# Two fused transformer blocks: the wide levels of a gated recurrence taken from keys and queries decayed once per chunk, and the key factor entered into the exponent as a logarithm

## The chip, the cores and the metric

The kernel runs on one core of one Trainium2 chip, as one program. Its engines work side by side and each takes its own instructions in the order of its own list: TensorE (PE; its weight loads are shown as PEld), VectorE (DVE), ScalarE (ACT), GpSimd (POOL) and SyncE (SP), which issues most transfers. The metric is the device time of one execution in microseconds (us), as the median over runs; smaller is better.

## The reference, cut to what matters

Two blocks of a transformer follow each other on 512 tokens of width 1024. The second block has a mixer with two halves: four heads of a gated recurrence (HGRN2, 128 features each) and eight heads of stick-breaking attention (64 features each).

```python
f = lbf + (1.0 - lbf) * sigmoid(f_logit)      # forget gate, per token and feature
k = 1.0 - f
bc = cumsum(log(f))                           # within chunks of 64 tokens
def step(state, inp):                         # one chunk
    qt, kt, vt, bt = inp
    decay = exp(where(causal, bt[t] - bt[s], -inf))
    a = einsum('td,sd,tsd->ts', qt, kt, decay)
    o_intra = a @ vt
    o_inter = (qt * exp(bt)) @ state
    b_last = bt[-1]
    new_state = exp(b_last)[:, None] * state + (kt * exp(b_last - bt)).T @ vt
    return new_state, o_intra + o_inter
```

The stick-breaking heads need `exp(log_sigmoid(z) + between)`, where `between` is a sum of logarithms taken backwards along the keys. Both halves are normalised per head, joined to `mixed`, and multiplied by `w_out`; a memory attention and a feed-forward layer follow.

## The kernel before

The kernel has no running state. For a head of the recurrence it writes the whole 512x512 matrix of scores as a sum over **levels**: at level hl the tokens are cut into blocks of 2*hl, and the scores of the upper half of a block against its lower half are one small product of decayed queries and decayed keys, both measured from the last token of the lower half. The levels are 1, 2, 4, 8, 16, 32 (inside a chunk), 64 (two neighbouring chunks), 128 and 256 (the wide ones, across chunks), and level 0 for the diagonal. `b` is the cumulative sum of log f within a chunk, written over `f` (tile q), with features on the 128 partitions and the 512 tokens along a row.

For a level up to 64, `exponents` (L1410) has POOL subtract for the lower half (L1417) and for the upper half (L1419), then `decayed` (L1400) has ACT take the exponential of the whole tile (L1407) and DVE multiply the lower half by the key factor kf (L1408) and the upper half by the query (L1409). For a wide level, `far_exponents` (L1431) first adds up chunk totals on POOL in single columns (L1438 to L1443), subtracts on POOL (L1448, L1450), and goes through the same exponential and products. `scores` (L1455) does the products on PE (L1460 for the diagonal, L1468 up to level 64, L1481 and L1487 for 128 and 256), and DVE and ACT fold the results into tiles that `hgrn_tail` (L1497) multiplies with the values.

Around this run the projections of the mixer ("fills": 256 columns of w_in each, three matmuls per product, since the weights and activations are split in a high part, cast on ACT at L403, and a low part, subtracted on DVE at L404), the stick-breaking heads (`sb_head`: PE L616, DVE L1556 to L1566, ACT L1560, L1561, L1567, transposes L756, products L1575), and the product with w_out (`fill_part`), which begins while the last two heads are still at their levels. `fill_part` splits four finished head outputs (tiles y) into high and low parts (tiles h) and then multiplies.

PE's order is written out by hand: `weave` (L653) goes through all of this as generators, asks a small planner with due times which step is ready (each step names its PE time and the chain of DVE, ACT and POOL work behind it, in `prepared`, `first` and `after`), and PE takes the steps in that order. `prepare` runs LOOK + 1 = 3 levels ahead of `scores`. The orders of DVE, ACT and POOL are chosen by the scheduler of the tile framework when the program is built, and are fixed from then on. Tiles w come from a pool of 16, PSUM banks b from a pool of 6.

Of the kernel before, what the change touches and what calls it, by code (L numbers as in the profile page):

```python
# [11 lines left out]
F32 = mybir.dt.float32  # L12
F32R = mybir.dt.float32r
U8 = mybir.dt.uint8
AF = mybir.ActivationFunctionType
ALU = mybir.AluOpType
AX = mybir.AxisListType

P = 128
S = 512  # L20
D = 1024
# [9 lines left out]
LEVELS = (32, 16, 8, 4, 2, 1)  # L31
# [63 lines left out]
def transformer_blocks_kernel(  # L95
# [41 lines left out]
    V, A, G, T = nc.vector, nc.scalar, nc.gpsimd, nc.tensor  # L137

    cp = ctx.enter_context(tc.tile_pool(name="cp", bufs=1))
# [7 lines left out]
    def nm(s):  # L147
        uid[0] += 1
        return f"{s}_{uid[0]}"
# [13 lines left out]
    def wt(dt=F32):  # L163
        return big("w", WBUFS, dt)
# [7 lines left out]
    def col(n=4, bufs=20):  # L172
        return sp.tile([P, n], F32, tag=f"c{n}", bufs=bufs, name=nm("c"))
# [383 lines left out]
    with tc.high_priority(2 * WPRIO):  # L557
        pre = PreNorm("mix_pre")
        with in_order({}):
            rs = []  # L560
            for t in range(5):
                if t < 4:
                    su = [squares(xt[t, 0]), col(1)]
                    V.tensor_tensor_reduce(out=junk2, in0=xt[t, 1], in1=xt[t, 1], scale=1.0 / D, scalar=0.0,
                                           op0=ALU.mult, op1=ALU.add, accum_out=su[1])
# [646 lines left out]
    for hl in (64,) + LEVELS:  # L1212
        nb = 64 // hl
# [15 lines left out]
    V.memset(ones_sb, 0.0)  # L1229
    V.memset(ones_sb[0:64, 0:64], 1.0 / 64)  # L1230
    V.memset(ones_sb[64:128, 64:128], 1.0 / 64)
    small = cp.tile([P, 2], F32, name="small")
    V.memset(small[:, 0:1], 1e-30)
    V.memset(small[:, 1:2], 1e-6)
    tiny, eps6 = small[:, 0:1], small[:, 1:2]


    def pools(first, second, mid):
# [145 lines left out]
    def hgrn_chain(hd):  # L1384
        q, f = store["q", hd], store["f", hd]
        yield STEP()
        kf = wt()
        A.activation(kf, f, AF.Copy, scale=-1.0, bias=1.0)
        A.activation(f, f, AF.Ln, bias=tiny)
        b = f  # L1390
        V.tensor_tensor_scan(out=b, data0=reset, data1=f, initial=0.0, op0=ALU.mult, op1=ALU.add)

        bc = b.rearrange("p (c t) -> p c t", t=64)
        tot = bc[:, :, 63]

        def halves(t, hl):
            v = t.rearrange("p (b u c) -> p b u c", u=2, c=hl)
            return v[:, :, 0, :], v[:, :, 1, :]

        def decayed(e, hl):  # L1400

            el, eu = halves(e, hl)
            if hl == 64:
                A.activation(el, el, AF.Exp)
                A.activation(eu, halves(b, hl)[1], AF.Exp)
            else:
                A.activation(e, e, AF.Exp)  # L1407
            V.tensor_tensor(el, el, halves(kf, hl)[0], op=ALU.mult)  # L1408
            V.tensor_tensor(eu, eu, halves(q, hl)[1], op=ALU.mult)  # L1409

        def exponents(hl):
            e = wt()
            el, eu = halves(e, hl)
            bl, bu = halves(b, hl)
            nb = 256 // hl
            ref = bl[:, :, hl - 1:hl].to_broadcast([P, nb, hl])
            G.tensor_tensor(el, ref, bl, op=ALU.subtract)  # L1417
            if hl != 64:
                G.tensor_tensor(eu, bu, ref, op=ALU.subtract)  # L1419
            decayed(e, hl)  # L1420
            return e

        ad = wt()

        w0, w13, w2 = [wt(F32R) for b in range(2)], [wt(F32R) for b in range(2)], wt(F32R)
        w2 = [w2[:, :256], w2[:, 256:]]

        def diagonals(t):
            return t.rearrange("p (a c) -> p a c", c=P)[:, 0:4:3]

        def far_exponents(hl):  # L1431
            nch = hl // 64
            nb = 256 // hl
            lowc, upc = col(8), col(8)
            tv = tot.rearrange("p (b u c) -> p b u c", u=2, c=nch)
            lv = lowc[:, :4].rearrange("p (b c) -> p b c", c=nch)
            uv = upc[:, :4].rearrange("p (b c) -> p b c", c=nch)
            G.tensor_copy(lv[:, :, nch - 1], tv[:, :, 0, nch - 1])  # L1438
            G.memset(uv[:, :, 0:1], 0.0)
            for c in range(nch - 1):  # L1440
                G.tensor_tensor(lv[:, :, nch - 2 - c], lv[:, :, nch - 1 - c],
                                tv[:, :, 0, nch - 2 - c], op=ALU.add)
                G.tensor_tensor(uv[:, :, c + 1], uv[:, :, c], tv[:, :, 1, c], op=ALU.add)  # L1443
            e = wt()
            ev = e.rearrange("p (b u c t) -> p b u c t", u=2, c=nch, t=64)
            bv = b.rearrange("p (b u c t) -> p b u c t", u=2, c=nch, t=64)
            for bb in range(nb):
                G.tensor_tensor(ev[:, bb, 0], lv[:, bb].unsqueeze(2).to_broadcast([P, nch, 64]),  # L1448
                                bv[:, bb, 0], op=ALU.subtract)
                G.tensor_tensor(ev[:, bb, 1], uv[:, bb].unsqueeze(2).to_broadcast([P, nch, 64]),  # L1450
                                bv[:, bb, 1], op=ALU.add)
            decayed(e, hl)
            return e

        def scores(hl, e):  # L1455
            ps = aux()
            if hl == 0:
                for gg in range(4):
                    sl = slice(gg * P, (gg + 1) * P)
                    T.matmul(ps[:, sl], kf[:, sl], q[:, sl], start=True, stop=True)  # L1460
                V.tensor_tensor(ad.rearrange("p (g t) -> p g t", g=4),
                                ps.rearrange("p (g t) -> p g t", g=4),
                                ident.unsqueeze(1).to_broadcast([P, 4, P]), op=ALU.mult)
                return 0.43
            if hl <= 64:
                for gg in range(4):
                    up = e[:, gg * P:(gg + 1) * P].rearrange("p (b u c) -> p b u c", u=2, c=hl)[:, :, 1, :]
                    T.matmul(ps[:, gg * 64:(gg + 1) * 64], e[:, gg * P:(gg + 1) * P], up,  # L1468
                             start=True, stop=True)
                V.copy_predicated(  # L1470
                    halves(ad, hl)[1],
                    masks[hl].rearrange("p (b c) -> p b c", c=hl),
                    ps[:, :256].rearrange("p (b c) -> p b c", c=hl))
                if hl == 1:
                    split(w0[0][:, :P], w0[1][:, :P], ad[:, :P])
                    split(*[diagonals(t) for t in w13], ad.rearrange("p (a c) -> p a c", c=P)[:, 1:4:2])
                    split(w2[0][:, :P], w2[1][:, :P], ad[:, 256:256 + P])
                return 0.21
            if hl == 128:
                for bb in range(2):  # L1480
                    T.matmul(ps[:, bb * P:(bb + 1) * P], e[:, bb * 256:bb * 256 + P],  # L1481
                             e[:, bb * 256 + P:bb * 256 + 256], start=True, stop=True)
                for bb, t in enumerate((w0, w2)):
                    split(t[0][:, P:256], t[1][:, P:256], ps[:, bb * P:(bb + 1) * P])
            else:
                for bb in range(2):
                    T.matmul(ps[:, bb * 256:(bb + 1) * 256], e[:, bb * P:(bb + 1) * P],  # L1487
                             e[:, 256:512], start=True, stop=True)
                split(w0[0][:, 256:], w0[1][:, 256:], ps[:, :256])
                split(w13[0][:, P:384], w13[1][:, P:384], ps[:, 256:])  # L1490
            return 0.22 if hl == 128 else 0.86

        order = (0, 64) + LEVELS + (128, 256)
        es = {0: None}

        def prepare(n):
            if n < len(order):  # L1497
                hl = order[n]
                es[hl] = far_exponents(hl) if hl > 64 else exponents(hl)

        def prepared(n):
            if n >= len(order):
                return ()
            far = order[n] > 64
            return (("G", 2.3),) * far + (("G", 0.7), ("G", 0.7)) * (not far) + (("A", 0.55), ("D", 0.7))

        first = (("A", 0.6), ("A", 0.6), ("D", 0.6))
        for n in range(1, LOOK + 1):
            prepare(n)
            first += prepared(n)  # L1510
        yield STEP(ops=(first,), lat=TLAT[2], need=1)
        for n, hl in enumerate(order):
            prepare(n + LOOK + 1)
            pe = scores(hl, es.pop(hl))
            after = {0: (("D", 0.6),), 1: (("D", 0.35), ("A", 0.7), ("D", 0.75)), 128: (("A", 0.32), ("D", 0.4)),
                     256: (("A", 0.55), ("D", 0.7))}.get(hl, (("D", 0.35),))
            last = n == len(order) - 1
            yield STEP(pe=pe, ops=(after, prepared(n + LOOK + 1)), lat=HLAT, need=int(not last), free=1,
                       back=0 if last else HBACK)
        store["w", hd] = w0, [t[:, :384] for t in w13], w2, [t[:, 384:] for t in w13]  # L1520
# [352 lines left out]
```

## Time and profile before

| | us |
|---|---|
| median of 3 runs | 1911.21 |
| lowest, highest | 1910.41, 1911.87 |
| the profiled execution's own time | 1912.74 |
| its span, first to last instruction | 1911.0 |
| PE busy over the span | 1881.5 (98%) |
| DVE, ACT, POOL busy over the span | 1388.6, 929.8, 174.9 |

The recurrent heads are worked on between about 1205 and 1410 us of the span. A matmul is counted as busy from its start to its modelled end, and matmuls overlap, so PE's busy share says little on how fast it moves; the time from one start to the next does. In a row of the timeline the first number is the start, the second the duration, and idle time ahead of an instruction stands in brackets with what ended it.

### The profile page before, as it was taken

The numbers are of one execution on the slowest core, as the hardware profiler recorded it, in microseconds if no ns is written. First come the engines' busy times: TensorE is split into PE (matmuls) and PEld (weight loads), VectorE is DVE, ScalarE is ACT, GpSimd is POOL, SyncE is SP. The second block draws the span as 40 slices with busy tenths as digits, with TensorE's granted clock in tenths as the row PEclk, the third lists the DMA queues.
The fourth block names the chain that finished last, engine by engine and source line by source line (L and its number), as shares of the span: only waits on it lengthen the run. The fifth ranks groups of instructions, "written<-read, shape, count | busy, mean of one in ns | idle before, by whom it ended". The sixth has DMA issues, their size and how long they took to land.

```text
span 1911.0 us, 29337 instructions
## 1 busy us (share of the span) xinstructions
PE 1881.5 (98%) x11566; PEld 1688.3 (88%) x11566; DVE 1388.6 (73%) x2217; ACT 929.8 (49%) x1537; POOL 174.9 (9%) x272
## 2 busy tenths in 40 slices
PE   8999999999999999999999999999999999999998
PEld 6899888888999998899999988888888778999997
DVE  6777635468878786777877757888976448878785
ACT  5666534364544445443434356657565344344443
POOL 2330100060000002000000010430410000000000
PEclk9999999999999999999999999999999999999999
DMA  5212224452233324423232342121343222232322
GB/s 180 67 55 68 78 66 154 166 176 89 89 111 96 120 93 162 143 67 111 90 119 99 114 160 71 63 94 39 103 152 133 77 85 82 99 111 89 111 88 89
DMA packets 164908, 198.69 MB, mean 104 GB/s; under 512 B 7745, under 2 KB 131746, under 8 KB 164770
## 3 DMA queue, kind: packets, MB, share of 16 engines
q1 hardware_dynamic: 163202, 192.10, 30.8%
q0 software_dynamic: 1280, 4.20, 0.6%
q8 instruction: 91, 1.49, 0.3%
q10 hardware_dynamic: 288, 0.52, 0.1%
q14 instruction: 47, 0.39, 0.1%
HBM read 186.30 MB, written 10.49 MB: 103 GB/s over the span
## 4 chain that ended last, share of the span: by engine, by line
PE 87%; issue 5%; DVE 3%; ACT 2%; POOL 1%; DMA 1%; SPq 0%; POOLq 0%; DVEq 0%; ACTq 0%
PE b L372 15%; PE b L374 15%; PE b L373 15%; PE a L372 11%; PE a L374 11%; PE a L373 11%; PE a L514 4%; PE b L616 1%; DVE wl L404 1%; PE b L490 1%; PE b L756 1%; PE b L1468 1%; PE b L1774 1%; DMA q<-mact_d 0%; PE b L886 0%
## 5 line engine op out<-in xcount | busy, mean ns | idle before, releaser
L404 DVE TENSOR_TENSOR wl<-wr,wh 128x1024 fp32r<-128x1024 f32 (+1 forms) x381 | 463.0, 1218 | 272.9 <-ACT wh L403 266.4
L403 ACT CAST wh<-wr 128x1024 fp32r<-128x1024 f32 (+1 forms) x381 | 394.1, 1036 | 443.9 <-PE b L373 144.1
L372 PE MATMUL b<-wh,q 128*128 128x512 f32 x672 | 262.4, 390 | 0.0
L373 PE MATMUL b<-wl,q 128*128 128x512 f32 x672 | 262.0, 390 | 0.0
L374 PE MATMUL b<-wh,q 128*128 128x512 f32 x664 | 258.2, 389 | 0.0
L372 PE MATMUL a<-h,wh 128*128 128x512 f32 (+1 forms) x660 | 238.4, 361 | 0.0
L374 PE MATMUL a<-h,wl 128*128 128x512 f32 (+1 forms) x660 | 234.9, 356 | 0.0
L373 PE MATMUL a<-h,wh 128*128 128x512 f32 (+1 forms) x660 | 234.7, 356 | 0.0
L373 PE MATMUL b<-h,wh 128*128 128x256 f32 (+1 forms) x568 | 175.9, 310 | 0.0
L372 PE MATMUL b<-h,wh 128*128 128x256 f32 (+1 forms) x568 | 175.9, 310 | 0.0
L374 PE MATMUL b<-h,wl 128*128 128x256 f32 (+1 forms) x568 | 175.9, 310 | 0.0
L374 PEld LDWEIGHTS b<-wh,q 128*128 128x128 f32 x664 | 124.6, 188 | 26.6
L372 PEld LDWEIGHTS b<-wh,q 128*128 128x128 f32 x672 | 126.3, 188 | 24.6
L373 PEld LDWEIGHTS b<-wl,q 128*128 128x128 f32 x672 | 126.3, 188 | 24.3
L373 PE MATMUL a<-s,wh 128*128 128x256 f32 (+1 forms) x488 | 141.2, 289 | 0.0
L374 PEld LDWEIGHTS a<-h,wl 128*128 128x128 f32 x660 | 124.6, 189 | 18.3
L372 PEld LDWEIGHTS a<-h,wh 128*128 128x128 f32 x660 | 124.7, 189 | 17.9 <-issue 0.5
L373 PEld LDWEIGHTS a<-h,wh 128*128 128x128 f32 x660 | 124.7, 189 | 17.8 <-issue 0.5
L373 PEld LDWEIGHTS b<-h,wh 128*128 128x128 f32 x568 | 108.3, 191 | 5.6
L374 PEld LDWEIGHTS b<-h,wl 128*128 128x128 f32 x568 | 108.2, 191 | 5.6
L372 PEld LDWEIGHTS b<-h,wh 128*128 128x128 f32 x568 | 108.1, 190 | 5.6
L374 PE MATMUL a<-wh,h 128*128 128x256 f32 x368 | 106.6, 290 | 4.5 <-DVE h L404 4.5
(379 smaller groups left out, 4179.7 us busy)
## 6 DMA issues: line engine op xcount, KB each, us to landing
wr<-in_ffn_w_gu_dram SPq DMA_DIRECT2D x88, 512.0 KB
wr<-in_w_in_dram SPq DMA_DIRECT2D x68, 512.0 KB
wr<-in_ffn_w_down_dram SPq DMA_DIRECT2D x44, 512.0 KB
wr<-in_w_gate_dram SPq DMA_DIRECT2D x22, 512.0 KB
wr<-in_w_up_dram SPq DMA_DIRECT2D x22, 512.0 KB
wr<-in_w_down_dram SPq DMA_DIRECT2D x22, 512.0 KB
wr<-in_mem_w_kv_dram SPq DMA_DIRECT2D x16, 512.0 KB
wr<-in_w_out_dram SPq DMA_DIRECT2D x10, 512.0 KB
```

The lines of the kernel that those rows point to most:

```text
L372: T.matmul(ps, lh, rh, start=first, stop=False)
L373: T.matmul(ps, lh, rl, start=False, stop=False)
L374: T.matmul(ps, ll, rh, start=False, stop=last)
L403: A.copy(hi, src)
L404: V.tensor_tensor(lo, src, f32(hi), op=ALU.subtract)
L490: T.transpose(banks[k][:, t * P:(t + 1) * P], self.s[t, k // 4][:, (k % 4) * P:(k % 4 + 1) * P], ident)
L514: T.matmul(accs[m], lh, rh, start=c == 0 and n in (0, 2), stop=c == KT - 1 and n > 3)
L616: T.matmul(ps, lh[n], rh[n], start=n == 0, stop=n == 1)
L756: T.transpose(ps[:, o * P:(o + 1) * P], blk, ident)
L1468: T.matmul(ps[:, gg * 64:(gg + 1) * 64], e[:, gg * P:(gg + 1) * P], up, start=True, stop=True)
L1774: T.matmul(po, lh, rh, start=n == 0, stop=n == 5)
```

## The change

The key factor is no longer multiplied in. ACT takes log(kf) once per head, DVE subtracts it from b once (tile bk), and the lower half's exponent is taken from bk instead of b, so one exponential gives the decayed key and a level has one product on DVE, for the query.

Level 64 is now built in `decayed` from whole chunks: keys decayed to the end of their chunk (kd, one POOL subtraction of 512 columns, one exponential) and queries decayed from the start of theirs (q times exp(b), both in place). The wide levels multiply those by products of whole-chunk decays (`ways`, two short scans on DVE behind two copies on POOL), on DVE alone. The order of the levels moves 64 from behind the diagonal to behind level 1, and the planner's chains are rewritten to match.

```diff
-        kf = wt()
+        bk, kf = wt(), wt()
         A.activation(kf, f, AF.Copy, scale=-1.0, bias=1.0)
         A.activation(f, f, AF.Ln, bias=tiny)
+        A.activation(bk, kf, AF.Ln, bias=tiny)
         b = f
         V.tensor_tensor_scan(out=b, data0=reset, data1=f, initial=0.0, op0=ALU.mult, op1=ALU.add)
+        V.tensor_tensor(bk, b, bk, op=ALU.subtract)
...
-            G.tensor_tensor(el, ref, bl, op=ALU.subtract)
-            if hl != 64:
-                G.tensor_tensor(eu, bu, ref, op=ALU.subtract)
-            decayed(e, hl)
+            G.tensor_tensor(el, ref, halves(bk, hl)[0], op=ALU.subtract)
+            G.tensor_tensor(eu, bu, ref, op=ALU.subtract)
+            A.activation(e, e, AF.Exp)
+            V.tensor_tensor(eu, eu, halves(q, hl)[1], op=ALU.mult)
             return e
...
-        def far_exponents(hl):
...
+        def decayed():
+            kd = wt()
+            G.tensor_tensor(kd.rearrange("p (c t) -> p c t", t=64), tot.unsqueeze(2).to_broadcast([P, 8, 64]),
+                            bk.rearrange("p (c t) -> p c t", t=64), op=ALU.subtract)
+            A.activation(b, b, AF.Exp)
+            A.activation(kd, kd, AF.Exp)
+            V.tensor_tensor(q, q, b, op=ALU.mult)
+            ways = col(16, 4)
+            G.memset(ways, 1.0)
+            G.tensor_copy(ways[:, 0:4:2], tot[:, 1:6:4])
+            G.tensor_copy(ways[:, 5:8:2], tot[:, 2:7:4])
+            for dst, src in ((ways[:, 8:11][:, ::-1], tot[:, 1:4][:, ::-1]), (ways[:, 13:16], tot[:, 4:7])):
+                V.tensor_tensor_scan(out=dst, data0=src, data1=zero.to_broadcast([P, 3]), initial=1.0,
+                                     op0=ALU.mult, op1=ALU.add)
+            base.append((kd, ways))
+            return kd
+        def far(hl):
+            nb, nch = 256 // hl, hl // 64
+            e, (kd, ways) = wt(), base[0]
+            ev, kv, qv = [t.rearrange("p (b u c t) -> p b u c t", u=2, c=nch, t=64) for t in (e, kd, q)]
+            o = 4 * nch - 8
+            for u, v in enumerate((kv, qv)):
+                w = ways[:, o + u * 4:o + u * 4 + 4].rearrange("p (b c) -> p b c", c=nch)
+                for bb in range(nb):
+                    V.tensor_tensor(ev[:, bb, u], v[:, bb, u], w[:, bb].unsqueeze(2).to_broadcast([P, nch, 64]),
+                                    op=ALU.mult)
             return e
...
-        order = (0, 64) + LEVELS + (128, 256)
+        order = (0,) + LEVELS + (64, 128, 256)
...
-            return (("G", 2.3),) * far + (("G", 0.7), ("G", 0.7)) * (not far) + (("A", 0.55), ("D", 0.7))
-        first = (("A", 0.6), ("A", 0.6), ("D", 0.6))
+            if order[n] > 64:
+                return ("D", 1.1),
+            if order[n] == 64:
+                return ("G", 1.3), ("A", 0.6), ("A", 0.6), ("D", 0.7)
+            return ("G", 0.7), ("G", 0.7), ("A", 0.6), ("D", 0.45)
+        first = (("A", 0.6), ("A", 0.6), ("A", 0.6), ("D", 1.2), ("D", 0.7))
```

The lists of DVE, ACT and POOL change between the first head and the end of the mixer, and so does PE's; outside of that stretch the engines' instructions are the same. From here on "the first, second, third and fourth head" are the four recurrent heads in their order.

The first place is DVE's list where `fill_part` begins. `h<-y` is the low part of a finished head output, `q<-reset,q` the cumulative sum of the fourth head, `q<-a` the low part of a value projection, `wl` that of weights. Before:

```order
L404 TENSOR_TENSOR h_13642<-y_12039,h_13641 128x512
L404 TENSOR_TENSOR h_13646<-y_12146,h_13645 128x512
L404 TENSOR_TENSOR wl_13762<-wr_13759,wh_13761 128x512
L404 TENSOR_TENSOR h_13650<-y_12138,h_13649 128x512
L404 TENSOR_TENSOR wl_13768<-wr_13765,wh_13767 128x512
L404 TENSOR_TENSOR q_13636<-a_13552,q_13635 128x256
L1556 SCALAR_TENSOR_TENSOR w_13602<-b_13601,consts 128x128
L1559 TENSOR_SCALAR w_13602<-b_13601 128x384
L404 TENSOR_TENSOR q_13636<-a_13552,q_13635 128x256
L404 TENSOR_TENSOR h_13654<-y_12880,h_13653 128x512
L1564 SCALAR_TENSOR_TENSOR w_13603<-ones_c,w_13603 128x512
L1391 SCALAR_TENSOR_TENSOR q_13107<-reset,q_13107 128x512
```

The same place in the changed kernel, from the second of the four on (L1395 is the new subtraction that gives bk, L1413 the product with the query for levels 32 and 16 of the fourth head):

```order
L404 TENSOR_TENSOR h_13609<-y_12147,h_13608 128x512
L404 TENSOR_TENSOR wl_13695<-wr_13692,wh_13694 128x512
L404 TENSOR_TENSOR q_13599<-a_13537,q_13598 128x256
L1393 SCALAR_TENSOR_TENSOR q_13080<-reset,q_13080 128x512
L404 TENSOR_TENSOR q_13599<-a_13537,q_13598 128x256
L1395 TENSOR_TENSOR w_13508<-q_13080,w_13508 128x512
L404 TENSOR_TENSOR h_13613<-y_12139,h_13612 128x512
L1563 SCALAR_TENSOR_TENSOR w_13587<-b_13586,consts 128x128
L1566 TENSOR_SCALAR w_13587<-b_13586 128x384
L1413 TENSOR_TENSOR w_13521<-w_13521,q_13186 128x8x32
L1413 TENSOR_TENSOR w_13526<-w_13526,q_13186 128x16x16
L404 TENSOR_TENSOR h_13617<-y_12824,h_13616 128x512
```

The cumulative sum of the fourth head, which stood behind the last of the four low parts, now stands between the second and the third, and two products of that head stand ahead of the fourth.

The second place is ACT's list at the same point, where `h<-y` is the high part (the cast). Before:

```order
L1560 ACTIVATE w_13530<-w_13529 128x384
L1561 ACTIVATE w_13530<-w_13530 128x384
L403 CAST h_13641<-y_12039 128x512
L403 CAST h_13645<-y_12146 128x512
L403 CAST wh_13761<-wr_13759 128x512
L1567 ACTIVATE w_13529<-w_13529 128x384
L403 CAST h_13649<-y_12138 128x512
L403 CAST wh_13767<-wr_13765 128x512
L403 CAST q_13635<-a_13552 128x256
L403 CAST h_13653<-y_12880 128x512
```

In the changed kernel (L1412 is the exponential of a level, here 32 and 16 of the third head; L1389 gives kf of the fourth head, L1390 and L1391 its two logarithms):

```order
L403 CAST h_13604<-y_12040 128x512
L1412 ACTIVATE w_13474<-w_13474 128x512
L1412 ACTIVATE w_13479<-w_13479 128x512
L403 CAST wh_13688<-wr_13686 128x512
L1389 ACTIVATE w_13509<-q_13080 128x512
L403 CAST h_13608<-y_12147 128x512
L403 CAST wh_13694<-wr_13692 128x512
L403 CAST q_13598<-a_13537 128x256
L1390 ACTIVATE q_13080<-q_13080,small 128x512
L1391 ACTIVATE w_13508<-w_13509,small 128x512
L403 CAST q_13598<-a_13537 128x256
L403 CAST h_13612<-y_12139 128x512
```

Two exponentials of the third head now stand between the first and the second cast, and the two logarithms of the fourth head between the second and the third.

The third place is PE's list at the end of the second head: L1487 and L1491 are its widest level, 256; the products into one bank b from tiles w and q are those with the values, `hgrn_tail`. Before, a projection (bank a) of 24 matmuls follows level 256, and the first eight rows are:

```order
L1481 MATMUL b_12869<-w_12760 128x128 x2
L1365 MATMUL b_12876<-w_12798,consts 128x512
L1365 MATMUL b_12882<-w_12853,consts 128x512
L1487 MATMUL b_12888<-w_12816 128x256 x2
L372 MATMUL a_12907<-h_11363,wh_12782 128x512
L373 MATMUL a_12907<-h_11364,wh_12782 128x512
L374 MATMUL a_12907<-h_11363,wl_12783 128x512
L372 MATMUL a_12907<-h_11367,wh_12782 128x512
```

In the changed kernel:

```order
L374 MATMUL a_12793<-h_11416,wl_12727 128x512
L1491 MATMUL b_12880<-w_12811 128x256 x2
L1366 MATMUL b_12887<-w_12857,consts 128x512
L372 MATMUL b_12905<-w_12233,q_12272 128x512
L373 MATMUL b_12905<-w_12234,q_12272 128x512
L374 MATMUL b_12905<-w_12233,q_12273 128x512
L372 MATMUL b_12905<-w_12235,q_12272 128x384
L373 MATMUL b_12905<-w_12236,q_12272 128x384
```

The products with the values now begin one matmul (a norm's, L1366) behind level 256, whose scores they need; before, a whole projection lay between.

## Rows read from the trace of the kernel before

**Rows 1.** The page's first part: busy us, share of the span, instructions.

```profile
PE 1881.5 (98%) x11566; PEld 1688.3 (88%) x11566; DVE 1388.6 (73%) x2217; ACT 929.8 (49%) x1537; POOL 174.9 (9%) x272
```

**Rows 2.** Windows: length, busy of PE, PEld, DVE, ACT, POOL, clock, DMA.

```profile
1205.00:1235.00 30.00, 29.43 (x197) 26.76 (x196) 22.84 (x38) 19.34 (x36) 17.09 (x38) 1.00 0.22 71
1235.00:1240.00 5.00, 3.31 (x20) 2.20 (x17) 4.84 (x10) 4.30 (x8) 2.05 (x3) 1.00 0.00 0
1240.00:1339.00 99.00, 99.00 (x609) 88.09 (x609) 83.82 (x161) 68.95 (x134) 18.62 (x37) 1.00 0.19 65
1339.00:1347.00 8.00, 4.07 (x22) 2.84 (x21) 6.94 (x13) 6.61 (x15) 0.00 (x0) 0.88 0.27 78
1347.00:1352.00 5.00, 5.00 (x26) 5.00 (x26) 4.81 (x6) 1.68 (x5) 2.41 (x4) 0.51 1.02 364
1352.00:1398.00 46.00, 46.00 (x380) 45.07 (x378) 41.22 (x84) 23.16 (x44) 24.64 (x44) 1.00 0.29 91
1398.00:1410.00 12.00, 11.16 (x75) 9.73 (x74) 9.37 (x22) 8.05 (x17) 0.00 (x0) 1.00 0.23 72
sum 205.00, PE 197.96 PEld 179.69 DVE 173.84 ACT 132.08 POOL 64.82; mean PE 28.28 PEld 25.67 DVE 24.83 ACT 18.87 POOL 9.26
```

**Rows 3.** Waits of PE, 1205 to 1410: total us, times, longest.

```profile
PE a L374 <- DVE h L404: 4.5, 4, 1.9
PE b L756 <- ACT w L1567: 1.4, 1, 1.4
```

**Rows 4.** Timeline of PE where fill_part begins: start, duration, instruction, idle before.

```profile
1339.45 0.63 PE L616 MATMUL b<-s,q 128*128 128x512 f32 x2
1340.34 0.38 PE L372 MATMUL a<-wh,h 128*128 128x256 f32 x1 [0.26 <-ACT h L403]
...
1346.35 0.58 PE L374 MATMUL a<-wh,h 128*128 128x256 f32 x1 [1.92 <-DVE h L404]
```

**Rows 5.** Timeline of DVE: the third head's cumulative sum.

```profile
1333.03 1.22 DVE L1391 TENSOR_TENSOR_SCAN q<-reset,q 128x512 f32<-128x512 f32 x1
```

**Rows 6.** Groups by form, 1205 to 1410: busy us, mean ns, idle before.

```profile
L1417 POOL TENSOR_TENSOR w<-q 128x256 f32<-128x256 f32 x28 | 21.6, 778 | 200.1 <-DVE q L1391 94.9 <-PE b L1365 72.3 <-PE b L1468 13.0
L1407 ACT ACTIVATE w<-w 128x512 f32<-128x512 f32 x32 | 20.1, 632 | 22.9 <-POOL w L1419 11.7 <-POOL w L1450 7.8 <-PE a L374 3.3
L1409 DVE TENSOR_TENSOR w<-w,q 128x256 f32<-128x256 f32 x36 | 19.8, 549 | 0.7 <-ACT w L1405 0.7
L1419 POOL TENSOR_TENSOR w<-q 128x256 f32<-128x256 f32 x24 | 19.5, 813 | 0.0
L1408 DVE TENSOR_TENSOR w<-w,w 128x256 f32<-128x256 f32 x36 | 19.2, 534 | 8.8 <-ACT w L1407 7.1 <-ACT w L1404 1.4
L1365 PE MATMUL b<-w,consts 128*128 128x512 f32 x16 | 8.2, 602 | 0.6 <-ACT w L1584 0.6
L1391 DVE TENSOR_TENSOR_SCAN q<-reset,q 128x512 f32<-128x512 f32 x4 | 4.8, 1212 | 0.0
L404 DVE TENSOR_TENSOR h<-y,h 128x512 fp32r<-128x512 f32 x6 | 4.1, 698 | 0.0
L403 ACT CAST h<-y 128x512 fp32r<-128x512 f32 x6 | 3.6, 613 | 2.3 <-PE a L373 1.5 <-DVE y L1588 0.8
L403 ACT CAST q<-a 128x256 fp32r<-128x256 f32 x8 | 2.9, 362 | 2.0 <-DVE q L404 2.0
L1389 ACT ACTIVATE q<-q,small 128x512 f32<-128x512 f32 x4 | 2.9, 714 | 0.0
```

**Rows 7.** Timeline: one DVE product with POOL at work, one with POOL idle.

```profile
1231.27 0.80 POOL L1417 TENSOR_TENSOR w<-q 128x256 f32<-128x256 f32 x1
1231.52 0.83 DVE L1409 TENSOR_TENSOR w<-w,q 128x256 f32<-128x256 f32 x1
...
1254.28 0.42 DVE L1409 TENSOR_TENSOR w<-w,q 128x256 f32<-128x256 f32 x1
```

**Rows 8.** Timeline of SP near the end of the mixer.

```profile
1412.34 0.50 SPq L1089 DMA_DIRECT2D q<-mact_d  x1
```

More of the change, by code (lines that the diff above doesn't have):

```diff
@@ L1231, in transformer_blocks_kernel @@
     V.memset(ones_sb[64:128, 64:128], 1.0 / 64)
-    small = cp.tile([P, 2], F32, name="small")
+    small = cp.tile([P, 3], F32, name="small")
     V.memset(small[:, 0:1], 1e-30)
     V.memset(small[:, 1:2], 1e-6)
-    tiny, eps6 = small[:, 0:1], small[:, 1:2]
+    V.memset(small[:, 2:3], 0.0)
+    tiny, eps6, zero = [small[:, k:k + 1] for k in range(3)]
     def pools(first, second, mid):
@@ L1398, in halves @@
             return v[:, :, 0, :], v[:, :, 1, :]
[L1400 to L1409, printed above, removed]
         def exponents(hl):
@@ L1429, in diagonals @@
             return t.rearrange("p (a c) -> p a c", c=P)[:, 0:4:3]
-        def far_exponents(hl):
[L1432 to L1452, printed above, removed]
@@ new lines, in hgrn_chain @@
+        base = []
+        def far(hl):
[8 more added lines that the diff above has]
+                                    op=ALU.mult)
@@ L1465, in scores @@
             if hl <= 64:
+                high = q if hl == 64 else e
                 for gg in range(4):
-                    up = e[:, gg * P:(gg + 1) * P].rearrange("p (b u c) -> p b u c", u=2, c=hl)[:, :, 1, :]
+                    up = high[:, gg * P:(gg + 1) * P].rearrange("p (b u c) -> p b u c", u=2, c=hl)[:, :, 1, :]
                     T.matmul(ps[:, gg * 64:(gg + 1) * 64], e[:, gg * P:(gg + 1) * P], up,
@@ L1473, in scores @@
                     ps[:, :256].rearrange("p (b c) -> p b c", c=hl))
-                if hl == 1:
+                if hl == 64:
                     split(w0[0][:, :P], w0[1][:, :P], ad[:, :P])
@@ L1498, in prepare @@
                 hl = order[n]
-                es[hl] = far_exponents(hl) if hl > 64 else exponents(hl)
+                es[hl] = far(hl) if hl > 64 else exponents(hl) if hl < 64 else decayed()
         def prepared(n):
@@ L1503, in prepared @@
                 return ()
-            far = order[n] > 64
-            return (("G", 2.3),) * far + (("G", 0.7), ("G", 0.7)) * (not far) + (("A", 0.55), ("D", 0.7))
-        first = (("A", 0.6), ("A", 0.6), ("D", 0.6))
+            if order[n] > 64:
[4 more added lines that the diff above has]
+        first = (("A", 0.6), ("A", 0.6), ("A", 0.6), ("D", 1.2), ("D", 0.7))
         for n in range(1, LOOK + 1):
@@ L1514, in hgrn_chain @@
             pe = scores(hl, es.pop(hl))
-            after = {0: (("D", 0.6),), 1: (("D", 0.35), ("A", 0.7), ("D", 0.75)), 128: (("A", 0.32), ("D", 0.4)),
+            after = {0: (("D", 0.6),), 64: (("D", 0.35), ("A", 0.7), ("D", 0.75)), 128: (("A", 0.32), ("D", 0.4)),
                      256: (("A", 0.55), ("D", 0.7))}.get(hl, (("D", 0.35),))
```

## The prediction

> **What bounds the kernel now.** I read the page's busy times first: PE is busy 98% of the span, DVE 73%, ACT 49%, POOL 9% [rows 1]. So an engine other than PE costs time only where PE waits for it, and the question is how much PE waits in the stretch that the change touches. The windows from 1205 to 1410 us answer that [rows 2]: PE is busy 197.96 of 205 us there, DVE 173.84, ACT 132.08, POOL 64.82, and the idle time lies in three places. Between 1235 and 1240 PE is busy 3.31 of 5 us; between 1339 and 1347 it starts 22 matmuls in 8 us; between 1398 and 1410 it is idle 0.84 us. The list of PE's waits [rows 3] names two releasers: the low parts h from DVE, 4.5 us in four waits, and one 1.4 us wait on the stick-breaking product of ACT (that is the place at 1235). No wait names a level's exponent, so the work that the change removes stands nowhere in front of PE.
>
> One more thing is to be seen in the windows. Right behind the long wait the granted clock is 0.51, the lower of its two levels, from 1347 to 1352, and 26 matmuls take 5 us, 0.192 each; between 1352 and 1398 at full clock 380 take 46 us, 0.121 each [rows 2]. The waits at `fill_part` cost twice, once as 8.0 − 22 × 0.121 = 5.3 us of lost starts and once as 26 × 0.071 = 1.8 us of slow matmuls: about 7.
>
> **The change part by part.**
>
> *Work taken away or added, beside PE.* DVE loses 72 products of 256 columns, 19.8 + 19.2 = 39.0 us [rows 6]. It gets 24 products for the query at 0.549 (13.2), four subtractions for bk and four products q times exp(b) of 512 columns at 0.698 as a low part has (5.6), 16 level-128 products of 128 columns and 8 of 256. No row shows those of 128 columns with a broadcast factor: they lie between nothing and 0.549, and I take half, 0.28 (4.4), with 8 × 0.549 (4.4). Eight scans of three columns lie between nothing and the 1.212 of a 512-column scan; I take 0.3 (2.4). Sum 30.0, 9 us less. POOL keeps 48 subtractions at 0.80 (38), gets four of 512 columns at twice 0.80 (6.4; between once and three times) and a dozen small ones (under 3): some 47 against 64.8, 18 less. ACT keeps 32 exponentials of 0.632, loses 8 of half the size (between 0.362, the cast of that width, and 0.632) and gets four logarithms at 0.714 [rows 6]: even within 2 us. All of it lies beside PE, whose instructions stay the same in number and kind, so by itself it is worth nothing; the price is in where it waits. In SP's list one reload for the memory attention, issued at 1412.34 [rows 8], moves behind a pair of weight loads at the very end: between nothing and 1 us, and I take nothing, for PE then has the rest of the mixer before it. The w tiles: bk and kd live through a head where kf did, one more of 16; DVE or POOL could wait for a free one, which I take as nothing and put in the last rival.
>
> *fill_part.* This is the large term. Before, PE comes to it at 1340.34 and gets the matmul that needs the last low part at 1346.35 [rows 4]. After, the last low part on DVE stands behind the fourth head's cumulative sum, its bk and its products for levels 32 and 16; the cumulative sum stands behind the logarithm on ACT, which stands behind the second cast, and that behind two exponentials of the third head, which wait for POOL. A chain over three engines has come in front of PE. I follow it from the third head's cumulative sum, which before begins at 1333.03 [rows 5]. After, a second logarithm and a stick-breaking scan come ahead of it; I put the end of its bk at 1338.8 (an estimate; from the old place it would be 1333.03 + 1.21 + 0.70 = 1334.9). Then POOL's subtraction 0.78 (its partner does not need bk and goes first), POOL's pair for level 16 at 1.6 beside the exponential of level 32, the exponential of level 16 at 0.63: 1341.8. ACT: a weight cast, kf and the second cast h at 0.61 each, 1343.6; another weight cast, 0.36 for q, the logarithm 0.71: 1345.3. DVE: cumulative sum 1.21, a 256-column low part 0.35 (half of 0.698), bk 0.70: 1347.6. POOL 0.8 and 1.6, ACT 0.63, DVE's last product 0.55 and at last the low part 0.70: 1351.9, with the durations of [rows 6]. Against 1346.35 that is 5.5 later. The bounds: if all the early part were in time, what is left hangs on PE's own value projection, whose end lies behind the matmul at 1339.45 [rows 4], about 1340.1; from there 0.36 + 0.35 + 0.70 + 0.8 + 1.6 + 0.63 + 0.55 + 0.70 = 5.7 gives 1345.8, 0.6 earlier than before. Upwards, two further POOL or ACT operations in the wrong place (0.8 + 0.63 each) make it 8. I take 5.5, since the queue orders say which instruction stands behind which. While the low part waits, everything behind it on DVE waits too: the stick-breaking scan and the next levels, for which PE has the rest of fill_part in hand. The slow clock behind the wait I leave at its 1.8 us; it could vanish or double.
>
> *The second head's end.* Before, 24 projection matmuls of 512 columns lie between level 256 and the products with the values (24 × 2 × 0.121, an estimate of 5.8 us). After, one norm matmul of 0.60 does. The products of the second group of rows need level 256's scores cast on ACT (0.36), with a low part on DVE (0.35), and ACT has a copy, two operations of the norm (one waits for that very norm matmul) and a cast in front: 0.6 + 3 × 0.63 + 0.36 + 0.36 + 0.35 = 3.6. PE covers that with the norm matmul and three to five products, 0.6 + 5 × 0.24 = 1.8. Loss 1.8; between nothing and 3.
>
> *Small ones.* The wait at 1235, idle 1.7 us, has one more product of the second head ahead of it: +0.5 (0 to 1). The norm matmul behind the stick-breaking tail comes earlier against its square: +0.4 (0 to 0.8). The idle 0.84 us behind 1398 goes, since the fourth head's last levels there now need DVE alone: −0.8 (0 to −0.84). What is late next there is the cast of the scores, which has the old place.
>
> Sum: 5.5 + 1.8 + 0.5 + 0.4 − 0.8 = 7.4. The profiled execution took 1912.74 with a span of 1911.0; it would take 1920.1. It lies 1.5 above the median of the runs shown, so the forecast on the median is 1911.2 + 7.4 = 1918.6.
>
> *A rule against this.* One product of 256 columns took 0.83 us on DVE while POOL subtracted, and 0.42 while POOL was idle [rows 7]; the mean of 36 is 0.549 [rows 6]. The Trainium skill, page "SBUF — State Buffer", section "Who interferes with whom", says that a VectorE instruction with two SBUF inputs contends with a GpSimd instruction that reads SBUF, and that whichever comes first holds the shared pair of ports to its end. The trace agrees in those two rows. By that rule 18 us less on POOL would free up to as much on DVE, twice my 9 us; as PE waits for DVE at one place only, this changes no term above but makes the second rival below likelier than the order alone would.
>
> **The rivals.**
>
> *Only what hangs on PE counts (no change).* The third head's early part is in time after all, as the scheduler saw it, and fill_part ends 0.6 earlier: −0.6 + 1.8 + 0.5 + 0.4 − 0.8 = +1.3, 1912.5. For it: POOL is busy only 17 of 30 us even in its densest stretch [rows 2]. Against it: the two exponentials now ahead of the second cast wait for POOL, where none did.
>
> *The waits go (faster).* The relief on DVE lets the low parts follow PE at once. Then the 5.3 at fill_part, the 1.8 of slow clock, the 1.7 at 1235 and the 0.8 at 1398 all go: −9.6, 1901.6. It decides if the last low part is ready before 1341. For it: DVE is busy 6.94 of the 8 us of that window [rows 2], so work taken off it there counts. Against it: the low part is behind more of the head's work, not less, and the chain from 1340.1 alone is longer.
>
> *A longer stall (slower still).* The fill_part chain takes its upper 8, the slow clock doubles (+1.8), the second head's end takes 3 and a wait for a w tile adds 1: 8 + 1.8 + 3 + 0.5 + 0.4 + 1 − 0.8 = +13.9, 1925.1. For it: the clock fell behind a 4.5 us wait before, and a 10 us one is longer. Against it: each step must come out at its bad end.
>
> **How the numbers follow.** The forecast has 0.52, no change 0.20, the waits that go 0.15, the longer stall 0.13. The forecast's own range is 1914 to 1922. For eight times in ten the range takes in the no-change case, most of the longer stall and the upper edge of the faster one: 1905 to 1925. About 0.2%, 3.8 us, is what a measurement of this kernel can tell from no change: below 1907.4 counts as faster, above 1915.0 as slower. Faster: the third case, and a little of the second, 0.17. Same: most of the second and the low edge of the forecast, 0.22. Slower: 0.61.
>
> **What would show it.** In the changed profile the waits of PE should name the low part h at fill_part with 9 to 12 us of lost starts instead of 5.3, with DVE's cumulative sum of the fourth head and two level products just ahead of the last low part, and a stretch at half clock behind it. The second head's products with the values should show a wait of 1 to 3 us on a low part of the scores. DVE should be busy about 9 us less and POOL 18 less over the mixer, with PE's busy count unchanged. The prediction is wrong if the last low part ends by 1346, or if the clock stays up.

## The result and the profile after

| | before | changed |
|---|---|---|
| median, us | 1911.11 (6 runs) | 1925.57 (6 runs) |
| lowest to highest | 1910.27 to 1913.03 | 1922.88 to 1927.17 |
| the profiled execution, its span | 1912.74, 1911.0 | 1926.3, 1924.6 |

The changed kernel is slower by a ratio of 1.0073, with a 95% interval of 1.0060 to 1.0086: 14.5 us, where 7.4 were forecast and the range ended at 1925.0. The direction was right, the size half of what came. The rival called "a longer stall" gave 1925.1, but for reasons that were only partly those that happened.

The work went as forecast. The page's first part of the changed kernel, to be held against [rows 1]:

```profile
PE 1886.5 (98%) x11566; PEld 1692.0 (88%) x11566; DVE 1381.5 (72%) x2210; ACT 927.9 (48%) x1533; POOL 158.4 (8%) x212
```

DVE lost 7.1 us (9 were forecast), POOL 16.5 (18), ACT 1.9 (even); PE has the same 11566 instructions. The sizes taken for operations that no row showed can now be read from the groups by form of the changed kernel, 1200 to 1425 us (mean ns behind the busy time):

```profile
L1428 POOL TENSOR_TENSOR w<-q,w 128x512 f32<-128x512 f32 x4 | 4.5, 1123 | 2.5 <-PE b L1472 2.0 <-DVE w L404 0.6
L1395 DVE TENSOR_TENSOR w<-q,w 128x512 f32<-128x512 f32 x4 | 3.3, 815 | 0.1
L1454 DVE TENSOR_TENSOR w<-w,c 128x128 f32<-128x128 f32 x8 | 2.6, 372 | 0.0
L1454 DVE TENSOR_TENSOR w<-q,c 128x128 f32<-128x128 f32 x8 | 2.5, 352 | 0.0
```

POOL's subtraction of 512 columns took 1.12 us (1.6 was taken), bk 0.82 (0.70), a 128-column product 0.36 (0.28). Of these only bk stands in a chain that PE waits for; the rest lies beside PE. Differences of this size do not explain the time.

PE's waits do. This is the list of them for the changed kernel, 1200 to 1425 us (total, times, longest), against [rows 3]:

```profile
PE a L374 <- DVE h L404: 4.2, 3, 2.9
PE a L372 <- ACT h L403: 4.2, 2, 2.5
PE b L756 <- ACT w L1574: 3.6, 1, 3.6
PE b L373 <- DVE w L404: 1.9, 3, 0.9
PE b L372 <- ACT w L403: 0.8, 1, 0.8
```

The first two are `fill_part`, the third is the stick-breaking transpose that waited 1.4 us before, and the last two, absent before, are the second head's products with the values (but for one wait of 0.4 us at 1422). The windows of the changed kernel around the three places show the rest (columns as in [rows 2]):

```profile
1224.00:1234.50 10.50, 8.43 (x51) 7.20 (x49) 8.35 (x13) 5.53 (x10) 7.53 (x10) 1.00 0.31 100
1234.50:1242.00 7.50, 6.01 (x25) 5.43 (x26) 5.14 (x11) 4.47 (x7) 0.16 (x1) 0.54 0.01 2
1275.00:1286.00 11.00, 9.22 (x45) 6.69 (x43) 7.54 (x14) 8.37 (x17) 0.00 (x0) 0.99 0.18 51
1286.00:1293.00 7.00, 6.49 (x20) 4.96 (x19) 1.55 (x4) 1.23 (x4) 0.00 (x0) 0.52 1.03 364
1338.00:1349.00 11.00, 11.00 (x91) 10.98 (x91) 7.55 (x12) 7.69 (x16) 1.81 (x3) 1.00 0.01 3
1349.00:1354.00 5.00, 1.65 (x8) 0.97 (x6) 3.63 (x7) 4.42 (x9) 1.04 (x2) 1.00 0.15 45
1354.00:1365.00 11.00, 5.88 (x26) 5.29 (x27) 9.75 (x14) 5.13 (x10) 7.78 (x9) 0.53 0.62 218
```

The granted clock is at its lower level three times in the mixer, once behind each of the three waits, where before it was there once. This is not the profiled execution alone: over the whole span the granted clock was 0.992 to 0.995 in the six runs of the changed kernel, and 0.995 to 0.998 in the runs of the kernel before that were timed beside the experiments below. Note that in such a stretch PE looks busy, 6.01 of 7.50 us, while it starts 25 instructions; the busy share hides it, the count and the clock show it.

To split the loss between places ("the account" from here on) I took, for each pair of neighbouring matmuls, the time from one start to the next less the usual time for that kind at full clock. What exceeds 0.2 us is put down as a wait; in a slow stretch, up to one more usual time is put down to the clock.

| place | before: waits, clock | changed: waits, clock | more | forecast |
|---|---|---|---|---|
| transposes near 1235 | 2.2, 0 | 3.7, 2.5 | 4.0 | 0.5 |
| second head's products with the values | 0.4, 0 | 3.6, 2.6 | 5.8 | 1.8 |
| fill_part | 4.6, 2.4 | 9.4, 2.0 | 4.4 | 5.5 |
| rest of the mixer | 3.4, 0 | 4.0, 0 | 0.6 | −0.4 |

The sum is 14.8; the spans differ by 13.6. The difference lies ahead of the mixer, in code that the change does not touch. In the profiled execution before, the clock also fell to its lower level between 95.8 and 99.2 us, and in the changed kernel's it did not. The windows, before and changed:

```profile
90.00:105.00 15.00, 14.66 (x111) 14.51 (x110) 10.12 (x29) 7.35 (x13) 7.53 (x10) 0.89 0.22 71
90.00:105.00 15.00, 14.66 (x118) 14.33 (x117) 11.62 (x30) 7.51 (x14) 7.38 (x8) 1.00 0.22 72
```

The same matmul of a projection starts at 1193.86 before and at 1192.55 in the changed kernel. So the changed kernel enters the mixer 1.3 us earlier and leaves it 13.6 us later: the mixer lost 14.9 us between these two executions, as the account has it.

The three places in PE's timeline of the changed kernel:

```profile
1231.94 0.49 PE L756 MATMUL b<-ident,w 128*128 128x128 f32 x3
1235.99 1.33 PE L756 MATMUL b<-ident,w 128*128 128x128 f32 x5 [3.56 <-ACT w L1574]
...
1282.54 0.50 PE L372 MATMUL b<-w,q 128*128 128x512 f32 x1
1283.97 0.50 PE L373 MATMUL b<-w,q 128*128 128x512 f32 x1 [0.93 <-DVE w L404]
1284.31 0.40 PE L374 MATMUL b<-w,q 128*128 128x512 f32 x1
1285.56 0.46 PE L372 MATMUL b<-w,q 128*128 128x384 f32 x1 [0.85 <-ACT w L403]
1286.53 0.69 PE L373 MATMUL b<-w,q 128*128 128x384 f32 x1 [0.52 <-DVE w L404]
...
1352.30 0.38 PE L372 MATMUL a<-wh,h 128*128 128x256 f32 x1 [2.53 <-ACT h L403]
...
1360.93 0.58 PE L374 MATMUL a<-wh,h 128*128 128x256 f32 x1 [2.87 <-DVE h L404]
```

At `fill_part` the last low part stands where the order said. DVE in the changed kernel, from the third low part on:

```profile
1353.83 1.22 DVE L1393 TENSOR_TENSOR_SCAN q<-reset,q 128x512 f32<-128x512 f32 x1
1354.96 0.40 DVE L404 TENSOR_TENSOR q<-a,q 128x256 fp32r<-128x256 f32 x1
1355.28 0.68 DVE L1395 TENSOR_TENSOR w<-q,w 128x512 f32<-128x512 f32 x1
1355.88 1.12 DVE L404 TENSOR_TENSOR h<-y,h 128x512 fp32r<-128x512 f32 x1
...
1358.18 0.79 DVE L1413 TENSOR_TENSOR w<-w,q 128x256 f32<-128x256 f32 x1 [0.52 <-ACT w L1412]
1359.38 0.42 DVE L1413 TENSOR_TENSOR w<-w,q 128x256 f32<-128x256 f32 x1 [0.41 <-ACT w L1412]
1359.72 1.16 DVE L404 TENSOR_TENSOR h<-y,h 128x512 fp32r<-128x512 f32 x1
```

Cumulative sum, bk, two products that wait for ACT (and ACT for POOL), and then the low part that PE needs at 1360.93: the chain of the prediction, step by step.

### The profile page after: what moved, and what is told of

It is laid out like the page before. It is cut to its first block, busy times and chain, and to the rows that moved or that the text cites. A ratio compares the mean times of both kernels' runs of the same rounds, so it can differ in the third digit from the quotient of the medians.

```text
span 1924.6 us, 29274 instructions
## 1 busy us (share of the span) xinstructions
PE 1886.5 (98%) x11566; PEld 1692.0 (88%) x11566; DVE 1381.5 (72%) x2210; ACT 927.9 (48%) x1533; POOL 158.4 (8%) x212
```

## The experiments

Two theories were put against each other. **Theory 1:** the order costs. The planner's new numbers for a head moved PE's steps, the queues of DVE and ACT followed, and PE now comes too early to three places, each with a stretch of slow clock behind it. **Theory 2:** the new work itself costs, since a logarithm and a subtraction now stand ahead of each head's first level. All kernels below were timed in five rounds against the kernel before, whose median lay between 1910.8 and 1911.4.

### The new work with the old planner numbers

```diff
-            if order[n] > 64:
-                return ("D", 1.1),
-            if order[n] == 64:
-                return ("G", 1.3), ("A", 0.6), ("A", 0.6), ("D", 0.7)
-            return ("G", 0.7), ("G", 0.7), ("A", 0.6), ("D", 0.45)
+            far = order[n] > 64
+            return (("G", 2.3),) * far + (("G", 0.7), ("G", 0.7)) * (not far) + (("A", 0.55), ("D", 0.7))
-        first = (("A", 0.6), ("A", 0.6), ("A", 0.6), ("D", 1.2), ("D", 0.7))
+        first = (("A", 0.6), ("A", 0.6), ("D", 0.6))
```

> The changed kernel's work with the old kernel's planner numbers (first, prepared); PE's list around the four heads is then in the old order. Theory 1 (the order is what costs: the new planner numbers moved PE's steps, and the queues behind them): the 10 us of new waits and the 5 us of slow clock go, 1908 to 1913. Theory 2 (the new work itself costs: one more logarithm and one more subtraction ahead of each head's first level): the waits stay at the heads' starts, 1918 to 1926.

1911.40 us, ratio 0.9997 (0.9988 to 1.0006): the whole loss is gone with the new work in place. Theory 2 is out. The windows of this kernel, over the stretches of [rows 2]:

```profile
1235.00:1240.00 5.00, 2.76 (x19) 2.49 (x19) 3.91 (x7) 4.16 (x7) 2.09 (x3) 1.00 0.00 0
...
1339.00:1347.00 8.00, 3.91 (x19) 2.67 (x18) 7.17 (x14) 6.65 (x14) 0.00 (x0) 0.85 0.29 73
...
sum 205.00, PE 197.88 PEld 180.66 DVE 168.00 ACT 131.70 POOL 47.41; mean PE 28.27 PEld 25.81 DVE 24.00 ACT 18.81 POOL 6.77
```

In the same 205 us DVE has 5.8 us less to do than before and POOL 17.4 less, and PE is busy as long (197.88 against 197.96). The saved work is worth nothing here: that is the other half of the result.

### The old work with the new planner numbers

The same lines, the other way round, in the kernel before.

> The old kernel's work with the changed kernel's planner numbers. Theory 1: the second head's products with the values again stand right behind its widest level, and PE waits there: 1917 to 1927. Theory 2: the old work has the short start of a head, so 1909 to 1914.

1931.37 us, ratio 1.0101 (1.0086 to 1.0117): slower still than the changed kernel, with none of its work (why by another 5.8 us was not tested). PE's waits in this kernel, 1200 to 1430 us:

```profile
PE a L374 <- DVE h L404: 6.4, 2, 5.6
PE b L1365 <- ACT w L1587: 4.8, 2, 4.2
PE a L372 <- ACT h L403: 3.9, 1, 3.9
```

The stall at `fill_part` is there again, 10.7 us by the same account, the second head's products wait 3.0, and the clock is low four times (9.2 us of cost). The two kernels together settle it: the loss comes with the new numbers, whichever the work.

### Which of the numbers

In the changed kernel, only `first` was put back:

```diff
-        first = (("A", 0.6), ("A", 0.6), ("A", 0.6), ("D", 1.2), ("D", 0.7))
+        first = (("A", 0.6), ("A", 0.6), ("D", 0.6))
```

> The changed kernel with one planner line of the old one: the chain ahead of a head's first level (first) at the old 1.8 us instead of 3.7. PE's list then has 24 projection matmuls between the second head's widest level and the products with the values again, and the four low parts at fill_part stand as before. If that line alone moved the steps: 1908 to 1913. If the new numbers for the levels (prepared) count as much: 1916 to 1922.

1912.79 us, ratio 1.0006 (0.9998 to 1.0015). With this one line put back, nearly all of the loss is gone; 1.7 us are left. The 24 projection matmuls stand behind level 256 again, and the products with the values wait for nothing but one low part (0.4 us).

The other way round, `first` new and `prepared` old:

> The other way round: the levels' planner numbers (prepared) are the old ones, the head's start keeps the new 3.7 us. PE's list has 12 projection matmuls (12 x 0.227 = 2.7 us) between the second head's widest level and its products with the values, and the low parts at fill_part stand as before. If the cover in front of the waits is what counts, the second head's end waits under 1 us and fill_part 4 to 5: 1912 to 1918, between the two. If the head's start line is harmless: 1908 to 1912.

1919.59 us, ratio 1.0044 (1.0032 to 1.0057). It came out above the 1912 to 1918 that were expected. With 12 matmuls of cover the second head's end was harmless as expected (0.8 us of waits and no slow clock from 1270 to 1300), but the moved steps met other queues elsewhere, at places that were not foreseen. PE's waits, 1200 to 1425 us:

```profile
PE b L756 <- ACT w L1571: 2.9, 2, 2.1
...
PE b L373 <- DVE w L404: 1.9, 1, 1.9
PE b L1491 <- DVE w L1454: 1.5, 1, 1.5
```

So the two sets of numbers do not simply add up: against the kernel before, the new `prepared` alone costs 1.7 us (just inside the noise), the new `first` alone 8.5, both together 14.5. PE's order shows why. Between the first and the second head's diagonal it has 6 projection matmuls before, 12 with only `first` put back, 18 with only `prepared` put back, and 72 in the changed kernel. Behind the second head's widest level it has 24, 24, 12 and 0.

### The stall at fill_part alone

In the changed kernel, the casts and low parts of `fill_part` get a priority; PE's list stays as it is.

```diff
-                for k in ks:
-                    msp[k] = halves_of(mixed[k], None, "h")
+                with tc.high_priority(CPRIO):
+                    for k in ks:
+                        msp[k] = halves_of(mixed[k], None, "h")
```

> The changed kernel, in which fill_part's casts and low parts get a higher priority; PE's list is the same, and the last low part stands ahead of the fourth head's cumulative sum. Theory 1: most of the stall at fill_part (9.4 us of waits and 2 us of slow clock in the changed kernel) goes, 4 to 8 us: 1918 to 1921. Theory 2: the low parts are late because ACT and DVE are behind with the new work, so at most 2 us: 1923.5 to 1926.

1920.24 us, 5.3 less than the changed kernel. The account gives 3.2 us of waits and 1.5 of clock at `fill_part` instead of 9.4 and 2.0; the other two places are as they were. So it is shown that the place of these casts and low parts in the queues makes this stall. The 5.3 us are not the size of what the change added there, since with the priority the place costs less (4.7 us) than it did before the change (7.0).

### Is it PE's idleness that lowers the clock?

In the changed kernel PE repeats one transpose inside the wait near 1235, writing the same values again:

```diff
         for o, blk in enumerate(jobs):
-            T.transpose(ps[:, o * P:(o + 1) * P], blk, ident)
+            for r in range(fillers.pop(0) if fillers and len(jobs) == 4 and o == 2 else 1):
+                T.transpose(ps[:, o * P:(o + 1) * P], blk, ident)
```

> The changed kernel, in which PE repeats one transpose 33 times more (33 x 0.109 = 3.6 us) inside the 3.7 us wait near 1232 to 1236; nothing else moves. If the clock falls because PE stands idle there, it stays up and the 2.5 us of half clock from 1234.7 to 1241.5 come back: 1922.5 to 1923.5. If it falls for another reason, 1925 to 1926.5.

1922.15 us, 3.4 less, a little more than expected, for work that computes nothing. PE's windows of this kernel, over the first four windows shown for the changed kernel:

```profile
1224.00:1234.50 10.50, 10.50 (x70) 9.39 (x69) 8.35 (x13) 5.55 (x11) 7.94 (x10) 1.00 0.32 101
1234.50:1242.00 7.50, 7.50 (x61) 7.07 (x60) 7.25 (x13) 4.38 (x7) 2.20 (x2) 1.00 0.00 0
1275.00:1286.00 11.00, 8.68 (x42) 6.25 (x41) 7.10 (x15) 7.14 (x14) 0.00 (x0) 1.00 0.35 114
1286.00:1293.00 7.00, 7.00 (x37) 5.65 (x36) 4.22 (x13) 3.50 (x7) 0.00 (x0) 1.00 0.75 276
```

From 1234.5 to 1242 PE has 61 instructions (17 of them repeats) instead of 25, at a clock of 1.00 instead of 0.54. The Trainium skill, "TensorE: Matmul & The Clock Gate", section "HAM oscillation — how this bites in real kernels", says that a wait for a DMA's data throws the engine back to the lower clock, so that the next piece of work starts slow; the waits here are for DVE and ACT, and these rows agree.

The 3.4 us are not the price of this one place, though. In this execution the clock also stayed up behind the second head's end, although the waits there were 3.1 us in sum, and stayed low longer at `fill_part` (13.7 us instead of 10.2). From one profiled execution to the other, matmul by matmul, the place near 1235 gives back 2.6 us, the second head's end 2.9, and `fill_part` costs 0.9 more. Why the clock differed at the two later places is not settled.

### Both together

> The changed kernel with both of its edits from before, the priority at fill_part (5.3 us in its run) and the 33 repeated transposes near 1235 (3.4 us in its run). If the loss is a sum of separate places: 1925.6 - 5.3 - 3.4 = 1917, 1915.5 to 1918. If one hides the other: 1919 to 1921.

1916.3 us (1914.0 to 1919.4), 9.3 less than the changed kernel where the two alone gave 8.7: the places add up. Of the 5.5 us that are left above the kernel before, the second head's end is the largest part: by the account of this kernel's profiled execution it has 3.4 us of waits and 1.4 of clock, against 0.4 before. No experiment treated that place alone. Near 1235 the repeats now fill the time of the wait, and `fill_part` costs 4.7 us against 7.0.

### Is there a version that beats both?

The priority at `fill_part`, raised to `2 * WPRIO`, on top of the old `first`:

> As after_firstold, and fill_part's casts and low parts get a high priority, so the last low part stands ahead of a weight's low part, a value's low part and a stick-breaking step. It should be ready 1.5 to 2 us earlier, and the half clock behind it (2.3 us before) shorten or go: 1907 to 1910. If the work put behind it is then waited for, no gain: 1911 to 1912.

1912.42 us, ratio 1.0004 (0.9995 to 1.0013), not the gain expected, and its runs spread from 1909.4 to 1913.5. The profiled execution, with a time of 1909.58, is one of its fastest. In it the wait for the last low part is 0.2 us (1.5 with only `first` put back), the stretch of slow clock behind it is half as long (3.4 us instead of 6.8), and the clock stays at 1.00 behind the 2.6 us wait near 1235; with only `first` put back, in its profiled execution, it fell there, from 1238.3 to 1241.7. Two fillers were tried on it. One of 24 transposes of the identity, ahead of `fill_part`'s first matmul:

> As firstold_splits, with 24 transposes of the identity (2.6 us) on PE ahead of fill_part's first matmul, inside its waits. If the waits stay as long and the clock stays up: 1 to 2.5 us below firstold_splits, 1905 to 1908. If the clock stayed up there anyway, or the filler delays the matmuls: the same or up to 2 us above it.

1915.36 us, ratio 1.0023 (1.0014 to 1.0032): 3 us worse. It shifted DVE's list, and PE met a new wait:

```profile
1359.93 0.58 PE L372 MATMUL a<-wh,h 128*128 128x256 f32 x1 [4.15 <-DVE s L1638]
```

The other, 23 repeats of the transpose near 1235, left all lists as they were:

> As firstold_splits, with 23 repeats of one transpose (23 x 0.109 = 2.5 us) inside the 2.6 us wait near 1235, so that PE does not stand idle there. firstold_splits spread from 1909.4 to 1913.5. If that spread is the clock falling behind this wait in some executions and not in others, the runs now draw together at the low end, 1908.5 to 1910, a median 2 to 3 us lower. If not, the median stays at 1911.5 to 1912.5.

1909.19 us (1908.7 to 1911.2), ratio 0.9992 (0.9983 to 1.0001). The runs drew together at the low end, as expected if the clock falls behind that wait in some executions: over the span the granted clock is 0.997 to 0.998 in all eleven runs, and was 0.995 to 0.998 without the repeats. The time cannot be told from that of the kernel before. And the kernel before with the same priority:

> The old kernel with the same high priority for fill_part's casts and low parts as in firstold_splits. If what that priority gives has nothing to do with the change's work: 1.5 to 3 us under the old kernel, 1908 to 1909.5. If it takes the DVE time that the change set free: 1911, no gain.

1908.59 us, ratio 0.9989 (0.9980 to 0.9997). This is the lowest median of all, 2.2 us below the kernel before, and it has none of the change. What could be had at `fill_part` was a matter of DVE's and ACT's order, not of their work.

## Why the prediction was wrong

**What bounds the kernel.** Right. PE's waits carried the time, and no level's exponent was among them. That the removed work lies beside PE and is worth nothing by itself was shown by the run with the old numbers, 0.9997. The rule that the prediction held against itself would have freed up to 18 us on DVE. DVE lost 7.1, and its 24 products with the query took 0.555 us each where they took 0.549 before, so this relief did not come.

**fill_part.** Right in mechanism and size: 5.5 forecast, 4.8 more of waits and 0.4 less of clock by the account. PE comes to it 8.9 us later than before (1349.26 against 1340.34) and gets the matmul that needs the last low part 14.6 later (1360.93 against 1346.35), so 5.7 of these arose inside. It was followed instruction by instruction from the order, with durations from rows. Only the start of the chain was an estimate without a row, the end of the third head's bk at 1338.8. It came at 1347.7, which is 8.9 later, as PE is. That estimate was exact without a row behind it, so the size owes something to luck.

**The slow clock.** This is the step that failed: "The slow clock behind the wait I leave at its 1.8 us; it could vanish or double." In its first windows the prediction had read that a wait at `fill_part` was paid twice, and it then priced the second payment only at that place. The two other waits, which it forecast itself to grow, got a slow stretch each, 2.5 and 2.6 us, where it had nothing. Together that is 5 of the missing 7 us. By place the account lies 3.5 above the forecast near 1235, 4.0 above it at the second head's end, 1.1 below it at `fill_part` and 1.0 above it in the rest. What the slow stretch costs is not fixed by the wait: behind the second head's end, with the same instructions on PE, it lasted 6.8 us in two profiled executions (the changed kernel and the one with the priority), 3.4 with the priority and the repeats together, and did not come with the repeats alone. The rival of a longer stall doubled the clock's cost at `fill_part`, where it did not grow.

**The second head's end.** The wait was seen, its cause too (no projection left between), but 1.8 was 3.2. The prediction followed one pair of cast and low part and set up to five products against it. There are two pairs, for 512 and for 384 columns of the products: PE waited for a low part at 1283.97, for a cast at 1285.56 and for another low part at 1286.53, each behind casts and low parts of weights or of a key projection of the stick-breaking heads, the second cast also behind two operations of the norm.

**The transposes near 1235.** Forecast 0.5 more for one product in front; the wait grew by 1.5. PE came there at 1231.94 instead of 1235.08, since a diagonal and a level of the second head (1229.16 to 1230.86 before) now stand behind the transposes. Of these 3.1 us, 1.3 are the earlier start of the whole mixer in this execution, which is not the change's doing; the chain that feeds the transposes was done only 1 us earlier (1235.99 against 1236.94), so PE came 1.8 us earlier and the chain was 0.4 us later. The diagonal's new place (it went from 1229.2 to 1250.4) was to be read from PE's order and was not worked out. DVE in the changed kernel in that stretch shows what the chain waits behind:

```profile
1229.89 0.98 DVE L1413 TENSOR_TENSOR w<-w,q 128x256 f32<-128x256 f32 x1 [1.23 <-ACT w L1412]
1230.91 0.68 DVE L407 SCALAR_TENSOR_TENSOR q<-a,q 64x512 fp32r<-64x512 f32 x1
1231.62 1.62 DVE L1571 TENSOR_TENSOR_SCAN w<-ones_c,w 128x512 f32<-128x512 f32 x1
1233.16 0.66 DVE L1464 TENSOR_TENSOR w<-b,ident 128x512 f32<-128x512 f32 x1
```

DVE waits 1.23 us for a level's exponential ahead of the stick-breaking scan, and a diagonal product stands behind it, all ahead of what the transposes need.

**The planner.** The prediction named the queues and took the planner's numbers as part of the change without asking which of them moves the steps. It is `first` above all, and the new `prepared` on top of it: the new 3.7 us of `first` come close to what the start of a head takes by the rows (kf 0.62, two logarithms at 0.72, the cumulative sum 1.22, bk 0.82, together 4.1), and the old 1.8 us do not. The truer number gave the worse order. A head that is said to start later gets projections put in front of it (72 matmuls instead of 6 ahead of the second head), and these are then missing at that head's end (0 instead of 24).

## What to carry to other kernels

When a change touches the numbers by which an order is planned, first run the new work with the old numbers and the old work with the new ones: here this pair separated 0 us of work from 14 to 20 us of order. Where a wait is forecast for an engine whose clock is granted, price the slow stretch behind it at every place, not only where the trace already shows one, and as a chance, since it came in some executions and not in others. Work that did not stand in front of the bounding engine was worth nothing when it was removed here, and what was rewritten to plan around its removal cost 14.5 us, through the order.

## What the runs showed of the hardware that was not expected

Useless transposes in a wait kept the clock at its upper level of 2.4 GHz there. The place gave back 2.6 us in the profiled execution, and the median fell by 3.4 (1925.57 to 1922.15). Near 1235, behind waits of much the same length (2.6 us by the account), the clock fell in one profiled execution and not in another. The kernel without the repeats there spread over 4.1 us (1909.4 to 1913.5), and with the wait filled its eleven runs lay within 2.6 us (1908.7 to 1911.2).

A wait is not all that decides. Between 95 and 99 us, in code that is the same in all kernels, the clock was at its lower level in 8 of the 13 profiled executions, with no wait of PE over 0.34 us from 75 us on; between the two profiles shown above it cost 1.5 us. The kernel before spread as widely (1909.8 to 1914.3 in 27 runs), so a spread alone does not point to one wait.
